# One two-bank PSUM place for the logits of a pair of heads, instead of three one-bank places

## The chip, the cores and the metric
The kernel runs on one core of a Trainium2 chip. The core has TensorE (PE, matrix products), VectorE (DVE), ScalarE (ACT) and GpSimd (POOL), each with its own queue of instructions that it takes in order, SyncE (SP) and other queues for transfers, and 16 DMA engines. Results of matrix products land in PSUM, eight banks of 128 partitions x 512 numbers of 32 bits, and are read from there by DVE or ACT. The metric is the device time of one execution in microseconds.

## The reference, cut to what matters
A sequence of 512 tokens of width 1024 passes through four layers, two of a first and two of a second kind.

```
for i in range(2):                     # first block
    a = gqa(q, k, v)                   # 4 query heads, 2 kv heads, 64 wide, all 512 keys
    b = bidirectional_ssd(...)
    c = softmax(q1 k1 + bias) v - lam * softmax(q2 k2 + bias) v   # 4 heads, 32 wide
    d = spatial_gating(...)
    x = x + merge(a, b, c, d, gates) @ w_out
    x = x + expert_choice_moe(x)       # 16 experts, 64 tokens each, 1024 wide
    x = x + sigmoid(x @ w_ple_gate) * (p @ w_ple)
for l in range(2):                     # second block, 8 heads of 64, causal
    s = sum_h iw[h] * relu(iq[h] . ik) # 4 index heads choose 128 keys a query
    a = softmax over the chosen keys
    b = window attention (128 keys back, 2 kv heads, a sink a head)
    c = stick breaking: beta[t,s] * prod_{s<j<t} (1 - beta[t,j])
    x = x + gate * (merge(a, b, c, gates) @ w_out)
return rms_norm(x)
```

All of it is float32. A projection is computed as three products of rounded halves (xh wh, xl wh, xh wl).

## The kernel before, in words
The program is written with tiles from pools. A pool has so many places under a tag (`bufs`); a tile that finds all places taken waits until the last reader of an earlier one is done, and the waits come from that by themselves. A scheduler sets the order on each engine: it follows the program's order as a priority, which `with self.ahead(n)` raises by n, and its own reckoning of when operands are ready. What it sets is fixed: at run time each engine takes its queue in that order, and an instruction that waits holds up those behind it.

The eight banks of PSUM are given out under three tags (L41 to L43, L122 to L129): `mm` three (projections, in the trace pj, pt, br, and experts), `at` two (transposes tp, products with v, small results), `lg` three, each with one 128x512 tile: the logits lg of the softmax attentions, z of the stick attention, ix of the index heads, and half of the experts' up-products.

Two heads of a pair j = 0, 1 lie on partitions 0 to 63 and 64 to 127 of one tile, so that a logits matmul has 64 rows. For a block of 128 queries (qb) each of these stages makes the logits of both heads, reads them from PSUM, forms the softmax or the sticks, transposes the probabilities (pn, sbb) by PE and multiplies them by v:
The grouped attention (gqa, L616 on; its q and k are qkT): logits over 512 keys, DVE's row maximum, ACT's exponential straight from PSUM. 8 pairs a layer.
The difference attention (L676 on; qks): the two maps m = 0, 1 of a head, 96 rows each (three products of 32 rows stacked); DVE's operation at L709 adds the bias, takes the maximum and writes e to memory. 32 matmuls a layer.
The selected and the window attention (soft_pair, L1492, called for both; names ak, aq and bk, bq): 128 to 512 and 128 to 256 keys; DVE reads them like that. 16 pairs a layer each.
The stick attention (L1594 on; ck, cq): 128 to 512 keys; ACT reads z twice (sba, sbb), POOL masks, DVE multiplies along the row. 16 pairs a layer.
The index scores (L1467 on): four heads for each of three query blocks, read by ACT.
The stages' work is interleaved by the scheduler with projections of stages before and after. The profile gives each PE operation the line of its helper (L153 for matmuls, L157 for transposes), so operations are told apart by the tiles' names.

## Time and profile before
| what | value |
|---|---|
| time, median of 3 runs (lowest to highest) | 3566.06 us (3564.95 to 3567.53) |
| profiled execution: its own time | 3565.2 us |
| its span, first to last instruction | 3563.5 us |
| mean granted clock of TensorE | 0.985 of full speed |
| busy: PE, DVE, ACT, POOL | 96%, 51%, 32%, 12% of the span |

A view by windows gives the busy time of each engine within a stretch of the span; a timeline gives single runs of like instructions (x4 means four records; a 64-row float32 matmul is recorded as two passes, so x2 is one and x4 are two of them). A run's duration is from the start of its first to the end of its last record, so that neighbours overlap a little. "PEclk" is the clock that PE was granted, 1.00 for 2.4 GHz and 0.50 for 1.2.

### The profile page before, as it was taken

Reading aid. Unit: us, or ns where it says so; the run is one execution under the profiler, and the core shown is the slowest. Engines: PE = TensorE matmul, PEld = TensorE weight load, DVE = VectorE, ACT = ScalarE, POOL = GpSimd, SP = SyncE. Lnnn points to the kernel's source line nnn. Section 1 sums busy time; section 2 is a strip of 40 time slices with the busy share of each in tenths; the row PEclk is TensorE's granted clock in tenths of the full one; section 3 lists DMA queues with packets and bytes.
Section 4 is the critical chain, followed back from the end, with each engine's and each line's share of the span. In section 5 each row is a group of like instructions: output and inputs, shape, how many; then the busy total and the mean of one; then the engine's idle time right before and its main releaser. Section 6 shows DMA issues by size and latency. Waiting matters only on the chain. (4 is left out here: it accounts for less than half of the span.)

```text
span 3563.5 us, 42081 instructions
## 1 busy us (share of the span) xinstructions
PE 3430.4 (96%) x15961; PEld 2298.0 (64%) x15961; DVE 1806.6 (51%) x3533; ACT 1133.5 (32%) x2209; POOL 419.1 (12%) x646
## 2 busy tenths in 40 slices
PE   8999999999999999999999999899999999999998
PEld 7867774443437877776434436676678877676887
DVE  7567652111117776673111115697644459756344
ACT  4344641000104444562000113225433322544333
POOL 0110421000000120151000000330210013103000
PEclk9999999999999999999999999899999999999999
DMA  5233667999993233465999985231123332221322
GB/s 177 73 88 108 199 216 282 385 387 388 376 378 109 66 111 105 149 231 202 388 373 402 380 353 226 71 101 62 46 76 103 102 116 76 79 71 36 107 95 71
DMA packets 315437, 655.97 MB, mean 184 GB/s; under 512 B 31075, under 2 KB 208575, under 8 KB 280931
## 3 DMA queue, kind: packets, MB, share of 16 engines
q1 hardware_dynamic: 291968, 628.78, 48.1%
q0 software_dynamic: 8192, 15.22, 1.7%
q10 hardware_dynamic: 15075, 9.29, 0.9%
q8 instruction: 126, 2.06, 0.2%
q14 instruction: 76, 0.62, 0.1%
HBM read 629.59 MB, written 14.70 MB: 181 GB/s over the span
## 5 line engine op out<-in xcount | busy, mean ns | idle before, releaser
L153 PE MATMUL pj<-xh,wh 128*128 128x512 f32 x1808 | 728.1, 404 | 14.3 <-DVE gb L150 6.4
L153 PE MATMUL pj<-xh,wl 128*128 128x512 f32 (+1 forms) x1808 | 725.1, 402 | 10.7 <-DVE wl L142 10.7
L153 PE MATMUL pj<-xl,wh 128*128 128x512 f32 (+1 forms) x1808 | 724.8, 401 | 0.9 <-DVE xl L150 0.7
L132 ACT ACTIVATE wh<-wst 128x1024 fp32r<-128x1024 f32 (+2 forms) x368 | 339.0, 930 | 754.2 <-PE pj L153 570.0
L142 DVE TENSOR_TENSOR wl<-wst,wh 128x1024 fp32r<-128x1024 f32 (+2 forms) x368 | 413.4, 1126 | 308.1 <-ACT wh L132 307.6
L153 PEld LDWEIGHTS pj<-xh,wh 128*128 128x128 f32 x1808 | 342.0, 189 | 110.0 <-DVE gb L150 9.6
L153 PEld LDWEIGHTS pj<-xh,wl 128*128 128x128 f32 (+1 forms) x1808 | 342.0, 189 | 102.7 <-DVE wl L142 13.7
L153 PEld LDWEIGHTS pj<-xl,wh 128*128 128x128 f32 (+1 forms) x1808 | 341.9, 189 | 94.2 <-issue 12.8
L153 PE MATMUL eg<-wst,xe 128*64 128x512 f32 x1008 | 293.0, 596 | 0.0
L153 PE MATMUL eg<-we,xe 128*64 128x512 f32 x560 | 228.4, 596 | 0.0
L153 PEld LDWEIGHTS eg<-wst,xe 128*64 128x64 f32 x1008 | 94.6, 136 | 134.1 <-issue 125.5
L142 DVE TENSOR_TENSOR x<-x,sct 128x512 f32<-128x512 f32 x128 | 83.8, 684 | 187.6 <-PE sct L153 187.6
L142 DVE TENSOR_TENSOR hd<-sg,eg 128x512 f32<-128x512 f32 x32 | 21.9, 685 | 309.0 <-PE eg L153 242.8
L153 PE MATMUL ey<-wst,ht 128*64 128x512 f32 x512 | 161.1, 599 | 7.4 <-DVE ht L139 3.9
L272 POOL TENSOR_TENSOR rr<-msb,mhalf 128x4 f32<-128x4 f32 x9 | 9.2, 1021 | 1344.9 <-DVE msb L146 1344.9
L153 PE MATMUL pt<-wh,xh 128*128 128x256 f32 x512 | 145.9, 285 | 1.4 <-DVE ro L142 1.2
L153 PE MATMUL pt<-wl,xh 128*128 128x256 f32 x512 | 145.1, 283 | 0.0
L153 PE MATMUL pt<-wh,xl 128*128 128x256 f32 x512 | 145.0, 284 | 0.0
L132 ACT ACTIVATE e<-e,nm 128x512 f32<-128x512 f32 (+3 forms) x192 | 111.2, 581 | 70.9 <-DVE nm L146 70.4
L1391 POOL TENSOR_TENSOR wada<-wada 128x1024 f32<-128x1024 f32 (+1 forms) x48 | 101.8, 2121 | 131.5 <-ACT wada L132 129.6
L153 PE MATMUL ey<-we,ht 128*64 128x512 f32 x256 | 115.3, 597 | 1.5 <-DVE ht L139 0.8
L153 PEld LDWEIGHTS eg<-we,xe 128*64 128x64 f32 x560 | 68.2, 136 | 74.2 <-issue 65.2
(495 smaller groups left out, 5788.9 us busy)
## 6 DMA issues: line engine op xcount, KB each, us to landing
wst<-in_w_in_dram SPq DMA_DIRECT2D x90, 1024.0 KB, 5.3
wst<-in_w_exp_gate_dram SPq DMA_DIRECT2D x66, 1024.0 KB, 8.6
wst<-in_w_exp_down_dram SPq DMA_DIRECT2D x64, 1024.0 KB, 11.1
wst<-in_w_exp_up_dram SPq DMA_DIRECT2D x60, 1024.0 KB, 7.8
wst<-in_w_branch_gate_dram SPq DMA_DIRECT2D x32, 1024.0 KB, 5.6
wada<-in_w_ada_dram SPq DMA_DIRECT2D x24, 1024.0 KB, 5.2
we<-in_w_exp_up_dram SPq DMA_DIRECT2D x88, 256.0 KB, 7.1
we<-in_w_exp_down_dram SPq DMA_DIRECT2D x80, 256.0 KB, 9.1
```

Of the source, the lines that this page charges most:

```text
L132: return self.nc.scalar.activation(out, in_, func, **kw)
L142: return self.nc.vector.tensor_tensor(out, a, b, op=op)
L153: return self.nc.tensor.matmul(out, lhsT, rhs, start=start, stop=stop, **kw)
L272: self.nc.gpsimd.tensor_tensor(r, ms, self.mhalf[:, :n], op=OP.pow)
L1391: nc.gpsimd.tensor_tensor(t[:, :k], t[:, :k], t[:, k:2 * k], op=OP.add)
```

## The change
The tag `lg` gets one place of two banks, and a function `lg2` that returns its two halves; `at` gets three places, so that PSUM holds 3 + 3 + 2 banks. The tiles that were single users of `lg` (the input's transposes, the transposes before the experts, those of the output) go to `at`. In the grouped, selected, window and stick attention and in the index scores the two matmuls of a pair are now written first, and both reads behind them; in the grouped and the stick attention with a raised priority (60 and 40). In the difference attention the two maps use the two halves, but stay written as matmul, read, matmul, read.

```diff
@@ -39,8 +39,8 @@
 NA = 10
 NP = 3
 NPM = 3
-NPL = 3
-NPA = 2
+NPL = 1
+NPA = 3
 
 
 def consts():
@@ -125,8 +125,10 @@
     def at(self, name):
         return self.ps.tile([P, S], FT, name=name, tag="at", bufs=NPA)
 
-    def lgp(self, name):
-        return self.ps.tile([P, S], FT, name=name, tag="lg", bufs=NPL)
+    def lg2(self, name):
+
+        t = self.ps.tile([P, 2, S], FT, name=name, tag="lg", bufs=NPL)
+        return t[:, 0], t[:, 1]
 
     def act(self, out, in_, func, **kw):
         return self.nc.scalar.activation(out, in_, func, **kw)
@@ -626,12 +628,12 @@
             for qb in range(NB):
                 es = []
                 mx, nm, ss, rs = (self.sa(n, 2) for n in ("mx", "nm", "ss", "rs"))
-                lg = []
+                lg = self.lg2("lg")
+                with self.ahead(60):
+                    for j in range(2):
+                        self.mat(lg[j], qkT[kv][j * 64:j * 64 + 64, qb * P:qb * P + P], qkT[2 + kv][j * 64:j * 64 + 64, :])
                 for j in range(2):
-                    ps = self.lgp("lg")
-                    self.mat(ps, qkT[kv][j * 64:j * 64 + 64, qb * P:qb * P + P], qkT[2 + kv][j * 64:j * 64 + 64, :])
-                    nc.vector.tensor_reduce(mx[:, j:j + 1], ps, axis=AX.X, op=OP.max)
-                    lg.append(ps)
+                    nc.vector.tensor_reduce(mx[:, j:j + 1], lg[j], axis=AX.X, op=OP.max)
                 self.ts(nm, mx, -0.125, OP.mult)
                 for j in range(2):
                     e = self.ae("e")
@@ -702,8 +704,9 @@
                     off = 384 - qb * P
                     es = []
                     mx, nm, ss, rs, r2 = (self.sa(n, 2) for n in ("mx", "nm", "ss", "rs", "r2"))
+                    lg = self.lg2("lg")
                     for m in range(2):
-                        ps = self.lgp("lg")
+                        ps = lg[m]
                         self.mat(ps, w[:, 0, m, qb * P:qb * P + P], w[:, 1, m])
                         e = self.ae("e")
                         nc.vector.tensor_tensor_reduce(e, ps, sv[:, j, 384 - off:896 - off][:, ::-1], scale, GONE, OP.add, OP.max, mx[:, m:m + 1])
@@ -1239,11 +1242,11 @@
                 side.append(lambda g4=g4, d2=d2, nx=nxt: gather(g4, d2, nx))
             xc = pr % 2 * P
             pss = []
-            for pool in (self.mm, self.lgp):
-                two = [pool("eg%d" % i) for i in range(2)]
+            for _ in range(2):
+                two = self.lg2("eu") if pss else [self.mm("eg%d" % i) for i in range(2)]
                 for k2 in range(4):
                     ts = [take() for j in range(2)]
-                    if pr == 0 and pool == self.mm:
+                    if pr == 0 and not pss:
                         gather(0, k2, xs)
                     for k in range(2):
                         kt = k2 * 2 + k
@@ -1474,9 +1477,11 @@
             nk = (qb + 1) * P
             acc = hold[:, qb * S - S:qb * S]
             for h in range(4):
-                ps = self.lgp("ix")
-                r = h % 2 * 64
-                self.mat(ps[:, :nk], iq[h // 2][r:r + 64, qb * P:qb * P + P], ik[r:r + 64, :nk])
+                if h % 2 == 0:
+                    two = self.lg2("ix")
+                    for j in range(2):
+                        self.mat(two[j][:, :nk], iq[h // 2][j * 64:j * 64 + 64, qb * P:qb * P + P], ik[j * 64:j * 64 + 64, :nk])
+                ps = two[h % 2]
                 t = self.ae("ixr")
                 self.act(t[:, :nk], ps[:, :nk], AF.Relu)
                 self.stt(acc[:, :nk], t[:, :nk], iw[:, qb * 4 + h:qb * 4 + h + 1],
@@ -1495,13 +1500,14 @@
         n = len(kts) * P
         mx, nm, ss, rs = (self.sa(x, 2) for x in ("mx", "nm", "ss", "rs"))
         es = []
+        lg = self.lg2("lg")
         for j in range(2):
             r = j * 64
-            ps = self.lgp("lg")
-            self.mat(ps[:, :n], q[r:r + 64, qb * P:qb * P + P], k[r:r + 64, kts[0] * P:kts[0] * P + n])
+            self.mat(lg[j][:, :n], q[r:r + 64, qb * P:qb * P + P], k[r:r + 64, kts[0] * P:kts[0] * P + n])
+        for j in range(2):
             e = self.ae("e")
             init = GONE if sink is None else sink[:, t * 2 + j:t * 2 + j + 1]
-            nc.vector.tensor_tensor_reduce(e[:, :n], ps[:, :n], mask, 0.125, init, OP.add, OP.max, mx[:, j:j + 1])
+            nc.vector.tensor_tensor_reduce(e[:, :n], lg[j][:, :n], mask, 0.125, init, OP.add, OP.max, mx[:, j:j + 1])
             es.append(e)
         self.ts(nm, mx, -1.0, OP.mult)
         for j in range(2):
@@ -1609,10 +1615,13 @@
             pts = [self.pt("ptc%d" % j) for j in range(2)]
             for qb in range(NB):
                 n = (qb + 1) * P
+                zz = self.lg2("z")
+                with self.ahead(40):
+                    for j in range(2):
+                        r = j * 64
+                        self.mat(zz[j][:, :n], q[t][r:r + 64, qb * P:qb * P + P], k[t][r:r + 64, :n])
                 for j in range(2):
-                    r = j * 64
-                    z = self.lgp("z")
-                    self.mat(z[:, :n], q[t][r:r + 64, qb * P:qb * P + P], k[t][r:r + 64, :n])
+                    z = zz[j]
                     a, b = self.ae("sba"), self.ae("sbb")
                     q1 = self.sb.tile([P, S + 4], FT, name="sbq", tag="ae", bufs=NA)
                     self.act(a[:, :n], z[:, :n], AF.Sigmoid, scale=-1.0)
```

The order on the engines shows what this does. First PE in the selected attention (lg from the tiles ak and aq, among projections pj and bv and transposes tp of the probabilities pn), before:

```order
L153 MATMUL lg<-ak_15497,aq_15493 128x256 [waits DVE_49]
L153 MATMUL bv<-xh,wl 128x512
L153 MATMUL bv<-xh,wh 128x512
L153 MATMUL lg<-ak_15497,aq_15493 128x384 [waits DVE_49]
L153 MATMUL bv<-xl,wh 128x512
L153 MATMUL bv<-xh,wl 128x512
L153 MATMUL pj<-xh,wh 128x512 [waits Activation_49]
L153 MATMUL pj<-xl,wh 128x512
L153 MATMUL pj<-xh,wl 128x512 [waits DVE_49]
```

and after:

```order
L155 MATMUL pj<-xl,wh 128x512
L155 MATMUL pj<-xh,wl 128x512
L155 MATMUL lg<-ak_15433,aq_15429 128x384 [waits DVE_49]
L155 MATMUL lg<-ak_15433,aq_15429 128x384
L155 MATMUL pj<-xh,wh 128x512
L155 MATMUL pj<-xl,wh 128x512
L155 MATMUL pj<-xh,wl 128x512
L155 MATMUL pj<-xh,wh 128x512
```

Single logits matmuls, each with a wait of its own for DVE, have become two in a row, of which only the first waits.

PE at the first head pair of the stick attention (z from ck and cq; tp of sbb are the transposes of the sticks), before:

```order
L153 MATMUL z<-ck_17758,cq_17754 128x256 [waits Activation_49]
L153 MATMUL z<-ck_17758,cq_17754 128x384 [waits Activation_49]
L157 MATMUL tp<-ident,sbb 128x128 [waits DVE_49,PE_49]
L153 MATMUL z<-ck_17758,cq_17754 128x384 [waits Activation_49]
L157 MATMUL tp<-ident,sbb 128x128 [waits DVE_49,PE_49]
L157 MATMUL tp<-ident,sbb 128x128 [waits DVE_49,Activation_49]
L157 MATMUL tp<-ident,sbb 128x128 [waits Pool_49]
L153 MATMUL z<-ck_17758,cq_17754 128x512
L157 MATMUL tp<-ident,sbb 128x128 [waits DVE_49,PE_49]
L157 MATMUL tp<-ident,sbb 128x128 [waits Pool_49]
L153 MATMUL z<-ck_17758,cq_17754 128x512 [waits Activation_49]
```

and after:

```order
L155 MATMUL z<-ck_17656,cq_17652 128x384 [waits Activation_49]
L155 MATMUL z<-ck_17656,cq_17652 128x384
L159 MATMUL tp<-ident,sbb 128x128 [waits DVE_49,PE_49] x3
L159 MATMUL tp<-ident,sbb 128x128 [waits Pool_49]
L155 MATMUL pj<-xh,wh 128x512
L155 MATMUL pj<-xl,wh 128x512
L159 MATMUL tp<-ident,sbb 128x128 [waits DVE_49,Activation_49]
L159 MATMUL tp<-ident,sbb 128x128 [waits Pool_49]
L155 MATMUL pj<-xh,wl 128x512
L155 MATMUL pj<-xh,wh 128x512
L155 MATMUL pj<-xl,wh 128x512
L155 MATMUL pj<-xh,wl 128x512
```

The two heads' z, which had transposes between them, stand together, and the wait for ACT (the reader of z) is on the first alone; projections (pj) stand between the transposes.

PE in the difference attention (lg from qks; pj and br are projections of the merge that runs beside it), before:

```order
L153 MATMUL lg<-qks 128x512 [waits DVE_49]
L153 MATMUL pj<-xh,wh 128x512 [waits Activation_49]
L153 MATMUL pj<-xl,wh 128x512
L157 MATMUL tp<-ident,pn 128x128 [waits DVE_49,PE_49]
L157 MATMUL tp<-ident,pn 128x128 x3
L153 MATMUL br<-odh,bh 128x512
L153 MATMUL lg<-qks 128x512 [waits DVE_49]
L153 MATMUL br<-odl,bh 128x512
```

and after:

```order
L155 MATMUL lg<-qks 128x512 [waits DVE_49]
L159 MATMUL tp<-ident,pn 128x128 [waits DVE_49,PE_49]
L159 MATMUL tp<-ident,pn 128x128 x3
L155 MATMUL lg<-qks 128x512 [waits DMASW3_49,DMASW2_49,DMASW6_49,DMASW1_49,DMASW7_49,DMASW0_49,DVE_49]
L155 MATMUL lg<-qks 128x512 [waits DVE_49]
L159 MATMUL tp<-ident,pn 128x128 [waits DVE_49,Activation_49]
L159 MATMUL tp<-ident,pn 128x128 x3
L155 MATMUL lg<-qks 128x512 [waits DVE_49]
```

At the change of head two logits matmuls now stand one behind the other, each with a wait for DVE. On DVE itself, in the same stage, the reads of the logits (e, mx from lg and the bias strip) with what stands around them, before:

```order
L146 TENSOR_SCALAR pn<-e,rs 128x512
L709 ISA e,mx<-lg,strip 128x512
L709 ISA mx 128x1
L150 SCALAR_TENSOR_TENSOR pn<-e,r_2624,pn 128x512 [waits DVE_49]
L709 ISA e,mx<-lg,strip 128x512
L709 ISA mx 128x1
```

and after:

```order
L148 TENSOR_SCALAR pn<-e,rs 128x512
L712 ISA e,mx<-lg,strip 128x512 [waits PE_49]
L712 ISA mx 128x1
L152 SCALAR_TENSOR_TENSOR pn<-e,r_2615,pn 128x512 [waits DVE_49]
L712 ISA e,mx<-lg,strip 128x512 [waits PE_49]
L712 ISA mx 128x1
```

The order is the same; the two reads had no wait for PE there, since both matmuls were known to be done, and each has one now.

## Rows read from the trace of the kernel before

**Rows 1.** The page: span and busy times of the engines.
```profile
span 3563.5 us, 42081 instructions
PE 3430.4 (96%) x15961; PEld 2298.0 (64%) x15961; DVE 1806.6 (51%) x3533; ACT 1133.5 (32%) x2209; POOL 419.1 (12%) x646
```

**Rows 2.** Windows by stage: window, length, PE, PEld, DVE, ACT, POOL, PEclk, DMA, GB/s.
```profile
195.00:245.00 50.00, 49.84 (x218) 29.68 (x218) 33.67 (x74) 23.76 (x52) 3.55 (x7) 1.00 0.16 45
275.00:390.00 115.00, 112.67 (x516) 86.86 (x516) 92.43 (x214) 56.39 (x115) 1.67 (x1) 1.00 0.40 130
557.00:1078.00 521.00, 506.83 (x2128) 217.60 (x2125) 89.63 (x152) 52.92 (x89) 0.31 (x1) 1.00 0.95 375
2296.00:2384.00 88.00, 81.17 (x432) 67.81 (x430) 85.23 (x192) 17.14 (x26) 28.45 (x44) 0.96 0.28 83
2384.00:2443.00 59.00, 58.26 (x270) 36.04 (x270) 43.59 (x148) 30.40 (x84) 5.92 (x9) 1.00 0.16 47
2443.00:2523.00 80.00, 79.59 (x398) 53.91 (x398) 55.70 (x208) 42.18 (x129) 0.15 (x1) 1.00 0.24 79
2549.00:2606.00 57.00, 53.70 (x236) 27.70 (x236) 48.70 (x85) 33.59 (x86) 29.65 (x95) 0.94 0.00 1
2556.70:2563.50 6.80, 6.45 (x19) 3.35 (x21) 5.49 (x10) 3.18 (x9) 3.70 (x11) 0.50 0.00 0
```

**Rows 3.** Timeline of PE, single runs of logits: start, duration, operation.
```profile
200.05 1.13 PE L153 MATMUL lg<-qkT,qkT 64*128 64x512 f32 x4
...
221.69 1.12 PE L153 MATMUL lg<-qkT,qkT 64*128 64x512 f32 x2
...
2445.90 0.48 PE L153 MATMUL lg<-bk,bq 64*128 64x128 f32 x2
...
2447.68 0.70 PE L153 MATMUL lg<-bk,bq 64*128 64x256 f32 x2
...
2451.72 0.70 PE L153 MATMUL lg<-bk,bq 64*128 64x256 f32 x4
...
2553.33 0.91 PE L153 MATMUL z<-ck,cq 64*128 64x384 f32 x2
```

**Rows 4.** Windows of tile lg alone: grouped (two layers), before, selected, window attention.
```profile
195.00:245.00 50.00, 12.26 (x32) 3.93 (x32) 10.79 (x16) 11.56 (x32) 1.00 0.16 45
1299.00:1347.00 48.00, 11.90 (x32) 3.63 (x28) 10.77 (x16) 11.54 (x32) 1.00 0.16 46
2347.00:2384.00 37.00, 0.92 (x6) 0.52 (x6) 0.01 (x1) 0.00 (x0) 1.00 0.29 82
2384.00:2443.00 59.00, 18.52 (x60) 7.50 (x60) 13.27 (x30) 0.00 (x0) 1.00 0.16 47
2443.00:2523.00 80.00, 17.08 (x63) 7.73 (x62) 14.91 (x34) 0.00 (x0) 1.00 0.24 79
```

**Rows 5.** Windows of tile z alone, stick attention of two layers.
```profile
2549.00:2606.00 57.00, 22.43 (x64) 8.16 (x64) 0.00 (x0) 24.86 (x64) 0.00 (x0) 0.94 0.00 1
3207.00:3264.00 57.00, 22.92 (x64) 8.53 (x64) 0.00 (x0) 24.84 (x64) 0.00 (x0) 0.94 0.00 1
```

**Rows 6.** Timeline of PE: projections behind a logits matmul.
```profile
2390.93 0.50 PE L153 MATMUL pj<-xh,wl 128*128 128x512 f32 x1
2391.27 0.40 PE L153 MATMUL pj<-xh,wh 128*128 128x512 f32 x1
2391.50 0.39 PE L153 MATMUL pj<-xl,wh 128*128 128x512 f32 x1
```

**Rows 7.** Timeline of PE: a logits matmul of the difference attention.
```profile
288.24 0.40 PE L153 MATMUL lg<-qks 96*128 96x512 f32 x1
```

**Rows 8.** Timeline of DVE in the difference attention, between two reads.
```profile
286.49 0.75 DVE L150 SCALAR_TENSOR_TENSOR pn<-e,r,pn 128x512 f32<-128x512 f32 x1
287.15 0.68 DVE L709 CUSTOM_DVE_ANT_0 e<-lg,strip 128x512 f32<-128x512 f32 x1
```

**Rows 9.** Waits, 2549 to 2606: who for whom, total, times, longest.
```profile
PEld z L153 <- issue: 3.3, 12, 0.8
```

More of the change, by code (lines that the diff above doesn't have):

```diff
@@ L395, in setup @@
         for k in range(KT):
-            ps = self.at("xps") if k % 2 else self.lgp("xps")
+            ps = self.at("xps")
             for tb in range(NB):
@@ L1152, in moe @@
             for tb in range(NB):
-                ps = self.lgp("h2t")
+                ps = self.at("h2t")
                 for k in range(4):
@@ L1681, in final @@
         for tb in range(NB):
-            self.copy(o[0][:, tb], turn(0, tb, self.lgp("ops")))
+            self.copy(o[0][:, tb], turn(0, tb, self.at("ops")))
         r = self.rms_cols()
-        pss = [turn(1, tb, self.mm("opm") if tb % 2 else self.lgp("ops")) for tb in range(NB)]
+        pss = [turn(1, tb, self.mm("opm") if tb % 2 else self.at("ops")) for tb in range(NB)]
         for tb in range(NB):
```

## Prediction
> **What bounds the kernel now.** I read the page's busy times first: TensorE (PE) is busy 3430.4 of 3563.5 us, VectorE (DVE) about half of that [rows 1]. A share of the whole span hides stages with different limits, so next come windows cut by stage [rows 2]. In their order: the grouped attention (195 to 245), the difference attention (275 to 390), the experts (557 to 1078), the index scores with their top-k (2296 to 2384), then in the second block the selected attention (2384 to 2443), the window attention (2443 to 2523) and the stick-breaking attention (2549 to 2606). The reader is to see three limits. In the attention stages PE is busy all but a little of the time and DVE has room: there a shorter PE program is a shorter kernel. The experts run with the DMA engines busy 0.95: PE time is worth nothing there. In the index stretch DVE works 85.23 of 88 us: it decides. The stick stage is its own case: PE 53.70 of 57, DVE 48.70, and in 6.8 us of it PE runs at half clock (1.2 GHz), last row of [rows 2].
>
> Then I looked at single logits matmuls on PE [rows 3]. A head has 64 rows, so two heads of a pair stand on different halves of the partitions. Two matmuls of 512 columns that follow each other (x4: each is recorded as two passes) take 1.13 us; one alone (x2) takes 1.12. At 256 columns it is 0.70 for two and 0.70 for one. So a pair runs side by side and costs what one costs. With three single places most second heads wait for a place of their own and come later, alone: that is what the change can take away.
>
> **What is removed: lone logits matmuls.** In the order of PE after the change the second matmul stands directly behind the first with no wait in 16 of 16 pairs of the grouped attention's two layers, 32 of 32 of the window attention, 30 of 32 of the selected and 28 of 32 of the stick attention. The sums per layer, from the durations of [rows 3] (0.48 for 128 columns, 0.70 for 256, 0.91 for 384, 1.12 for 512):
> Grouped attention: 8 pairs x 1.13 = 9.0 instead of 12.26 and 11.90 [rows 4]: 3.2 + 2.9 = 6.1 us for both layers.
> Selected and window attention: now 0.92 + 18.52 + 17.08 = 36.5 [rows 4]. After: 4 x (0.48 + 0.70 + 0.91 + 1.12) + 0.70 for a split pair = 13.5, and 4 x 0.48 + 12 x 0.70 = 10.3. Saved 12.7 a layer, 25.3 in two.
> Stick attention: now 22.43 and 22.92 [rows 5]. After: 4 x 3.21 + 1.18 for two split pairs = 14.0. Saved 8.4 and 8.9, 17.3.
> Sum 48.7 us, all of it on an engine that these stages wait for.
>
> **Fewer changes of shape.** Behind a 64-row matmul the next projection matmul starts, and the one behind it starts 0.34 us later, where the usual step is 0.23 [rows 6]: about 0.1 us is lost each time PE leaves a run of such matmuls. In PE's order these runs fall from 158 to 118: 40 x 0.1 = 4 us saved. Bounds 0 and 40 x 0.2 = 8.
>
> **What moves.** With `ahead` the scheduler issues the stick logits earlier than their program order, and it moves projection work into the stick stage: in PE's order the stage grows from 132 to 213 instructions. PE has 57 - 53.70 = 3.3 us idle in it [rows 2], in two layers 6.6; with projections at hand between pairs I count it as filled. Bounds 0 and 6.6. The half-clock windows (3.4 us lost in each of two layers, if at full clock the same work needed half of 6.8) may stay or vanish; PE was waiting in short steps before the clock fell, and I take 0, bounds 0 and 7 gained.
>
> **What is added: a wait.** One place for two logits means that the first matmul of a pair waits until the last read of the pair before. Where both matmuls are issued together I let projections cover that wait: they stand between the pairs in PE's order. The difference attention is different. Its code still issues matmul, read, matmul, read, its matmuls have 96 rows and don't pair, and the two halves of the place are watched as one: each matmul waits for the read just before it, where formerly it waited for the read three back. The chain from one read to the next is then: PE's issue after a wait, about 0.28 (3.3 / 12 [rows 9]), and the matmul 0.40 [rows 7], together 0.68, against 0.66 from 286.49 to 287.15 in which DVE works on the multiply-add between [rows 8]. The cover just fails; PE is moreover in the middle of another instruction of about 0.40, half of it on average 0.2. So 0.25 for each second read: 32 in two layers, 8 us. What is queued behind the waiting matmul on PE are projections and transposes that had nothing to wait for, and DVE has 23 us of room there, so I count the delay as PE's. Below: nothing, if PE always comes late anyway; above: every one of 64, 16 us. At the change of head two matmuls stand directly one behind the other, the second waiting for the read of the first (0.28 + 0.68): twice a layer, 4 us for the kernel.
> The places of the experts' up-products, of the transposes and of the final output change too. The experts are hidden by the DMA engines; the others are few: 0, bounds -3 and +3. The index pairs save PE time where DVE decides: 0, bounds -2 and +2.
>
> **Sum.** -48.7 - 4 - 6.6 + 8 + 4 = -47.3. Against the profiled execution's 3565.2 that is 3517.9; the median of the runs shown is 0.9 above it, so 3519.
>
> **The rivals.**
> First: the readers take over. The faster PE waits for the engines that empty PSUM. By rows, in the stick stage DVE has 48.70 us of work, and with 16 hand-offs of 0.28 it can't be shorter than 53.2: it gives 3.8 a layer instead of 8.6 + 3.3. That takes 16 of my 47 away: -31, 3535. For it: the single place ties logits to readers. Against it: in the other stages DVE is at 33.67 of 50, 43.59 of 59, 55.70 of 80 [rows 2], with 25% to spare. The Trainium skill, TensorEngine Tiling (Array Packing), Performance Considerations, has this as a rule: tiling speeds up TensorE but not the emptying of PSUM, which may become the bottleneck. By it the time is 3535; no row before the change shows a stage in which that has happened. Chance 0.2.
> Second: the change does not do what it says. The matmuls stand together but a write to the other bank of one place doesn't start beside the first. Then only the runs and the idle time are won, and the difference attention's 12 are lost: 3563 to 3567. Against it: pairs in the kernel before run side by side also from banks next to each other. 0.06.
> Third, slower: the wait at the hand-off. A pair can't start before the last read of the pair before is done, and PE, which takes its instructions in order, stands still until then. There are 112 hand-offs of pairs (16 + 32 + 32 + 32) and 64 in the difference attention. Without my 12 for the latter the gain is 59; shared by 176 hand-offs the point of decision is 0.34 us each. At 0.45 it costs 79, a loss of 20: 3585. Against it: one cycle of a pair fits well in its stage. In the stick stage four activations of 0.39 (24.86 / 64 [rows 5]), the pair of 0.9 and two hand-offs of 0.28 make 3.0, where 57 / 16 = 3.6 are to be had; in the grouped attention two reads and two exponentials of 0.7, the pair of 1.1 and three hand-offs make 4.8 of 6.3. 0.06.
> Fourth: more. The half-clock windows go (7), the difference attention is hidden (12): 3500. 0.15.
> My forecast has 0.53.
>
> **How the numbers follow.** The low end 3494 is the fourth case and the upper bounds of runs and small places; the high end 3552 holds the first rival with the difference attention at its upper bound (3535 + 8) and some 9 for pairs split by the clock's moves in time. Left out are the second and third rivals and a third of the fourth: 0.17. About 0.2% or 7 us is what a measurement of this kernel can tell from no change. Faster by more: 0.53 + 0.2 + 0.15 and none of the second, 0.88. The second gives nearly all of no change, 0.05; slower is the third and what is left, 0.07.
>
> **What would show it.** Right: 64-row logits in runs of x4 with the duration of a x2 now; the logits' PE time near 9 us in the grouped attention, 24 in selected and window together, 14 in stick; the end of the second block's attention some 21 us a layer earlier; the difference attention up to 6 us a layer longer with PE waiting for DVE's read at the logits. Wrong: lone x2 logits as frequent as now; PE idle before logits at the pairs, released by ScalarE's or DVE's reads; the stick stage no shorter than 53 us at equal content, with DVE without a gap; or the experts' stages changing at all.

## The result, and the profile after

The changed kernel takes 3508.69 us (median of 4 runs, 3505.55 to 3509.70), the kernel before 3565.51 in the same comparison: a ratio of 0.9838, 95% interval 0.9821 to 0.9855, 57 us faster. The forecast was 3519, 47 us faster. The total is close, but it is the sum of errors of opposite sign, and that they nearly cancel is luck: the experts' stages, which I put at nothing, gave 43 us, and the second block gave 28 of the 49 us that I put there (logits and filled idle time). The page after, which answers to [rows 1]:

```profile
span 3506.4 us, 42089 instructions
PE 3355.4 (96%) x15961; PEld 2274.0 (65%) x15961; DVE 1809.8 (52%) x3533; ACT 1133.2 (32%) x2209; POOL 422.3 (12%) x646
```

PE does the same 15961 records in 75 us less, and its idle time grows by 18 (133 us before, 151 after); the other engines do what they did. Where that falls is seen from the starts of operations that both traces have. Lengths of five stretches, first layer / second layer of their block, worked out from those starts (us):

```
stretch (from .. to)                                        before        after
M grouped attention .. router (first qkt to first rlg)    339.7/338.1   343.0/342.6   +7.8
E experts (first slt to the next norm's ms)               539.2/541.1   517.5/520.2  -42.6
I index and top-k (iwt to first bk)                       112.8/113.6   113.3/113.4   +0.3
A selected and window attention (first bk to first z)     177.3/177.5   163.8/164.5  -26.5
S stick attention and merges (first z to last merge / to output)
                                                          297.0/341.7   296.6/340.8   -1.3
everything else                                                                       +5.0
```

Two of these stretches do not hold the same work before and after. In each layer 35 records of a projection (pt, 4.9 us of PE) moved from A into S, so that at equal content A gained some 8 us a layer and S some 5.5. And 12 records of a projection (pj, 2.8 us) moved from each expert stage into the stretch behind it, so that E gained some 37 us at equal content.

**The logits did what was worked out.** Windows of the tiles lg and z alone on PE, columns as in [rows 4, 5]: grouped attention, selected with window attention, and stick attention of both layers.

```profile
193.00:243.00 50.00, 8.20 (x30) 2.11 (x28) 10.52 (x16) 11.55 (x32) 1.00 0.24 66
...
2318.00:2480.00 162.00, 23.72 (x128) 9.62 (x124) 27.57 (x62) 0.00 (x0) 1.00 0.25 75
```
```profile
2506.00:2564.00 58.00, 13.79 (x64) 5.10 (x62) 0.00 (x0) 22.84 (x62) 0.00 (x0) 1.00 0.06 19
3151.00:3209.00 58.00, 14.12 (x64) 5.39 (x64) 0.00 (x0) 22.59 (x62) 0.00 (x0) 1.00 0.06 19
```

23.7 us where 13.5 + 10.3 = 23.8 were predicted, 13.8 and 14.1 where 14.0 were, 8.2 where 9.0 were (two of the 32 records start before this window; all 32 take 9.03 in either layer). In PE's timeline the pairs now read x4 at the duration of the x2 in [rows 3]:

```profile
2423.89 0.70 PE L155 MATMUL lg<-bk,bq 64*128 64x256 f32 x4
...
2512.66 0.92 PE L155 MATMUL z<-ck,cq 64*128 64x384 f32 x4
```

**The stick stage.** Its window after, with the clock at 1.00 where it was 0.94:

```profile
2506.00:2564.00 58.00, 51.55 (x273) 30.80 (x271) 46.74 (x82) 31.52 (x85) 28.78 (x91) 1.00 0.06 19
```

It holds 37 records more than in [rows 2], since projections were moved in, and it isn't the same piece of work: from the first to the last z there are 47.6 us and 189 records before, 56.9 us and 270 records after. PE is idle for 58 - 51.55 = 6.5 us in it, where 3.3 were idle before and I had none left. ScalarE's wait for logits and PE's wait for the finished sticks (sbb) have grown; before, in 2549 to 2606:

```profile
ACT sba L132 <- PE z L153: 5.7, 9, 2.3
...
PE tp L157 <- DVE sbb L142: 2.1, 3, 0.9
```
and after, in 2506 to 2564:
```profile
ACT sba L134 <- PE z L155: 19.1, 14, 3.2
...
PE tp L159 <- DVE sbb L144: 5.7, 10, 1.3
```

So most of PE's idle time there, 5.7 of 6.5 us, ends with a stick that VectorE finished.

**The experts.** Their window, as in [rows 2], now moves 391 GB/s with the DMA engines 0.98 busy, against 375 and 0.95:

```profile
558.00:1058.00 500.00, 484.66 (x2120) 214.86 (x2119) 87.82 (x151) 52.56 (x88) 0.31 (x1) 1.00 0.98 391
```

PE's idle time in this window did not fall: 521 - 506.83 = 14.2 us before, 500 - 484.66 = 15.3 after. Its busy time fell, by 22 us at nearly the same records. Before the change PE hardly waited for weights either: in 557 to 1078 its weight loads waited 3.8 us in sum for transfers, the matmuls themselves never; the largest entry:

```profile
PEld eg L153 <- DMA wst<-in_w_exp_up_dram: 0.8, 3, 0.3
```

One part of what changed is read from the scatter products (sct: each expert result is multiplied into an `at` place, and VectorE adds it to x, L142 before, L144 after). Instruction groups by line (durations in ns as minimum/median/maximum, then the first and last start), and the waits of PE and of its weight loads for that addition; before:

```profile
L153 PE MATMUL sct<-oht,yh x64: 387/494/505, 613.2 to 1076.3; 128*128 128x512 f32 x64
...
PEld sct L153 <- DVE x L142: 10.9, 16, 1.2
...
PE sct L153 <- DVE x L142: 4.9, 12, 0.8
```
and after:
```profile
L155 PE MATMUL sct<-oht,yh x64: 388/400/506, 615.6 to 1055.7; 128*128 128x512 f32 x64
...
PEld sct L155 <- DVE x L144: 5.3, 10, 1.0
PE sct L155 <- DVE x L144: 0.6, 1, 0.6
```

From the first scatter to the last there are 463.1 us before and 440.1 after. PE's own wait for VectorE's addition is nearly gone, and PE is busy for less time with the same scatters (tile sct alone, 56 of the 64), before and after:

```profile
560.00:1050.00 490.00, 39.40 (x112) 18.22 (x112) 36.77 (x56) 1.00 0.96 379
```
```profile
560.00:1050.00 490.00, 34.69 (x112) 18.69 (x112) 35.74 (x56) 1.00 0.99 394
```

In steps from the start of one PE operation to the start of the next, worked out from the trace of the first layer, those that end at a scatter sum to 51.5 us before and 41.4 after: 10 of the stage's 21.7 us, half of them idle time. Another 10.7 lie in the steps of the gate and up products (246.7 us before, 236.0 after), of which 6.5 are lost again before the transposes of their results (hdt). Why those products step faster isn't shown. In PE's order the scatters of both layers stand in 65 runs, before in 84, and the expert products between them are cut into fewer pieces (144, before 162). The shorter scatter doesn't come from that: its median is 400 ns with three places (here and in e1) and 486 to 494 with two (before, e2, and e5 with 70 runs).

**The difference attention.** PE around one change of head, from the timeline with its idle time in brackets:

```profile
287.22 0.40 PE L155 MATMUL br<-odh,bl 128*128 128x512 f32 x1
288.33 0.49 PE L155 MATMUL lg<-qks 96*128 96x512 f32 x1 [0.71 <-DVE mx L712]
289.08 0.63 PE L159 MATMUL tp<-ident,pn 128*128 128x128 f32 x4 [0.26 <-DVE pn L152]
289.61 0.50 PE L155 MATMUL lg<-qks 96*128 96x512 f32 x1
293.29 0.80 PE L155 MATMUL lg<-qks 96*128 96x512 f32 x1 [3.18 <-DVE mx L712]
294.05 1.09 PE L159 MATMUL tp<-ident,pn 128*128 128x128 f32 x4
294.88 0.79 PE L155 MATMUL lg<-qks 96*128 96x512 f32 x1
295.63 0.79 PE L155 MATMUL pj<-xh,wh 128*128 128x512 f32 x1
```
```profile
293.20:299.20 6.00, 5.87 (x14) 3.67 (x15) 4.53 (x10) 3.52 (x6) 0.00 (x0) 0.52 0.07 25
```

The matmul at 289.61 is the second head's first map, the one at 293.29 its second. The second waits 3.18 us for VectorE to read the first, in the same place (3.78 us in the second layer; there is one such change of head a layer). VectorE has other work in its queue before that read, of the merge (bl, macc) and of the softmax of the pair before (from its timeline):

```profile
290.14 0.69 DVE L144 TENSOR_TENSOR bl<-wst,bh 128x512 fp32r<-128x512 f32 x1
290.75 0.69 DVE L144 TENSOR_TENSOR macc<-macc,gb 128x512 f32<-128x512 f32 x1
291.82 0.17 DVE L717 RECIPROCAL rs<-ss 128x2 f32<-128x2 f32 x1 [0.39 <-ACT e L134]
...
292.55 0.68 DVE L712 CUSTOM_DVE_ANT_0 e<-lg,strip 128x512 f32<-128x512 f32 x1
```

The hand-off itself is short: that read ends at 292.55 + 0.68 = 293.23, and the matmul starts at 293.29. Behind the idle stretch PE runs at half clock (0.52 granted in the next 6 us, second fence; 0.50 in the second layer): projections take 0.79 instead of 0.40. Over the stage the granted clock is 0.97, where [rows 2] has 1.00:

```profile
273.00:388.00 115.00, 109.22 (x481) 81.10 (x480) 87.82 (x205) 54.27 (x111) 1.67 (x1) 0.97 0.36 118
```

### The profile page after: what moved, and what is told of

It is laid out like the page before. It is cut to its first block, busy times and chain, and to the rows that moved or that the text cites. A ratio compares the mean times of both kernels' runs of the same rounds, so it can differ in the third digit from the quotient of the medians.

```text
span 3506.4 us, 42089 instructions
## 1 busy us (share of the span) xinstructions
PE 3355.4 (96%) x15961; PEld 2274.0 (65%) x15961; DVE 1809.8 (52%) x3533; ACT 1133.2 (32%) x2209; POOL 422.3 (12%) x646
## 4 chain that ended last, share of the span: by engine, by line
PE 66%; issue 16%; DVE 9%; POOL 3%; ACT 3%; DMA 2%; ACTq 0%; POOLq 0%; DVEq 0%; SPq 0%
PE pj L155 27%; PE ey L155 7%; PE eg L155 6%; PE eu L155 4%; PE br L155 4%; PE pt L155 3%; PE av L155 2%; PE xe L155 2%; PE tp L159 2%; PE lg L155 2%; PE sct L155 2%; DVE wl L144 1%; DVE sel L1492 1%; PE pw L155 1%; DVE m L1491 1%
## 5 line engine op out<-in xcount | busy, mean ns | idle before, releaser
L144 DVE TENSOR_TENSOR wl<-wst,wh 128x1024 fp32r<-128x1024 f32 (+2 forms) x368 | 415.5, 1132 | 290.7 <-ACT wh L134 288.5
L155 PEld LDWEIGHTS pj<-xh,wl 128*128 128x128 f32 (+1 forms) x1808 | 341.7, 189 | 95.9 <-DVE wl L144 10.7
L155 PEld LDWEIGHTS pj<-xl,wh 128*128 128x128 f32 (+1 forms) x1808 | 342.8, 190 | 93.9 <-issue 10.1
L144 DVE TENSOR_TENSOR hd<-sg,eu 128x512 f32<-128x512 f32 x32 | 21.9, 685 | 338.4 <-PE eu L155 225.5
L155 PE MATMUL eg<-wst,xe 128*64 128x512 f32 x528 | 158.1, 597 | 0.0
L144 DVE TENSOR_TENSOR x<-x,sct 128x512 f32<-128x512 f32 x128 | 81.2, 682 | 133.9 <-PE sct L155 133.9
L155 PE MATMUL eu<-wst,xe 128*64 128x512 f32 x480 | 130.6, 593 | 1.3 <-DMA wst<-in_w_exp_up_dram 1.3
L155 PE MATMUL eu<-we,xe 128*64 128x512 f32 x288 | 117.9, 593 | 0.2 <-DMA we<-in_w_exp_up_dram 0.2
L155 PE MATMUL eg<-we,xe 128*64 128x512 f32 x272 | 116.6, 598 | 0.0
```

The lines of the kernel that those rows point to most:

```text
L144: return self.nc.vector.tensor_tensor(out, a, b, op=op)
L155: return self.nc.tensor.matmul(out, lhsT, rhs, start=start, stop=stop, **kw)
```

## The experiments

Each run's time stands against runs of the kernel before on the same chip (3564 to 3566 us in all of them). The stretches M, E, A and S are those of the table above.

**e1: the third place alone.** The kernel before with
```diff
-NPL = 3
-NPA = 2
+NPL = 2
+NPA = 3
```


> The kernel before, with the third place for small results taken from the logits (logits two single places, no pairs written together). Theory A, a third place for small results shortens the experts' stages: the two expert stages lose 18 to 21 us each as in the changed kernel, while the attentions gain nothing, since singles stay singles: 3526 to 3540. Rival B, the two-bank place of the up-products did it: the expert stages keep their 540 us, and the whole stays at 3560 to 3580.

Measured: 3555.03 us, ratio 0.997 (0.9959 to 0.9981). E is 521.0/525.2: 34 us of the 43, with PE's wait at the scatters as short as in the changed kernel:
```profile
PEld sct L153 <- DVE x L142: 5.8, 10, 1.0
PE sct L153 <- DVE x L142: 0.9, 2, 0.5
```
The whole is slower than A's range, because the attentions with two single places lost 21 us (A 181.3/181.3, S 303.5/348.1). The third place for small results is the larger part of the experts' gain. The rest, some 4 us a layer, came only with the two-bank place; why was not tested, and e6 shows that an expert stage whose code is unchanged can differ by 2 to 6 us between two versions.

**e2: without the third place.** The changed kernel with
```diff
-NPA = 3
+NPA = 2
```


> The changed kernel with two places for small results instead of three (one bank unused). Theory A: both expert stages grow by 18 to 21 us, the attentions keep their gain: 3545 to 3553. Rival B: the expert stages stay short, 3507 to 3515.

Measured: 3549.24 us, ratio 0.9952 (0.9937 to 0.9967), 41 above the changed kernel, in A's range. E goes back to 537.8/534.6 (the 12 projection records of each stage go back too, 5.6 us of this), and the waits to 10.7 and 4.3. A is 168.0/167.4: the pairs keep 9 to 10 of their 13 us there with two places.

**e3: half of the scatters elsewhere.** The kernel before with
```diff
-            ps = self.at("sct")
+            ps = self.at("sct") if i % 2 else self.lgp("sct")
```


> The kernel before, with every other scatter product of the experts in a place of the logits (of whose three the experts use only two), nothing else changed. Theory A1, it is the scatter that waits for a place that VectorE is still reading: PE's time at the scatters falls from 47 to about 39 us a layer and the two expert stages shorten by 14 to 21 us each, 3525 to 3540. Rival A2, the third place works through the other small results or through how the scheduler groups the scatters (their runs on PE stay near 80 here, against 65 in the changed kernel): under 6 us a stage, 3555 to 3566.

Measured: 3571.12 us, ratio 1.0017 (1.0008 to 1.0027), E 536.8/538.6, which the 12 projection records that left each stage here too account for. A1 fell in this form: places lent from the logits' rotation, in which the up-products turn too, don't help, and PE's wait at the scatters stayed (5.0 us, before 4.9). A2's stages came true, the whole lies 5 us above its range. Why the lent place doesn't help is open; e10 and e11 show by another way that the scatters depend on their places.

**e4: pairs undone in two attentions.** The changed kernel with
```diff
             self.mat(lg[j][:, :n], ...)
-        for j in range(2):
             e = self.ae("e")
```


> The changed kernel, in which the selected and the window attention are again written as matmul, read, matmul, read, in the two-bank place. Theory, lone matmuls cost their full time on a PE that decides: the logits of the two stages rise from 24 to 37 us a layer or more, and with a hand-off before every matmul another 0 to 10 us a layer: 3531 to 3550. Rival, the stages have slack on PE and pairing there bought nothing: 3506 to 3514.

Measured: 3568.19 us, ratio 1.0013 (1.0004 to 1.0023): 59 above the changed kernel, and above both theories' ranges. A is 197.2/195.9, 33 us a layer longer. The window of lg alone, first layer:
```profile
2352.00:2550.00 198.00, 45.78 (x120) 18.03 (x119) 28.50 (x60) 0.00 (x0) 0.96 0.17 54
```
All 64 logits matmuls are alone now; at the durations of [rows 3] that is 2 x (12.84 + 10.32) = 46.3 us, as measured, against 23.7 in pairs. So 22 of the 33 us are the pairs; of the rest 3 are more idle time on PE, and what remains lies in slower projections and products around (the clock fell to 0.96 here). One place without pairs is worse than three single places without them (A 177.3): the change pays by its order and the place together.

**e5: scatters in twos, two places.** The kernel before with
```diff
-                for d in range(4):
-                    side.append(lambda i=dh * 4 + d, ...: scatter(i, yh, yl, oht))
+                for d in range(0, 4, 2):
+                    side.append(lambda i=dh * 4 + d, ...: [scatter(i + u, yh, yl, oht) for u in range(2)])
```


> The kernel before, with the experts' scatter products written two at a time between the steps of the weights instead of one at a time; places unchanged. On PE the runs of scatters fall from 84 to 70 (65 in the changed kernel), the pieces into which they and the others cut the expert products from 162 to 154 (144). Theory G, each cut of the expert products costs PE, whatever the number of places: the two expert stages (539 and 541 us) shorten by 8 to 15 us each, 3535 to 3550. Rival P, what cost was the scatter's wait for a place that VectorE still reads: two at a time need two places at once, so PE's idle time before scatters grows from 5.8 us a stage and the stages shorten by 0 to 4 us or lengthen, 3557 to 3575.

Measured: 3555.23 us, ratio 0.9975 (0.9964 to 0.9987), E 537.1/533.4: 2.1 and 7.7 us shorter. Below G in both layers, and between the two ranges as a whole; the waits for the addition stayed (10.1 and 4.5 us). Fewer cuts alone are worth little, if anything, not the 20 us: untouched stages differ by up to 6 us in e6.

**e6: both maps of the difference attention first.** The changed kernel with
```diff
                     for m in range(2):
+                        self.mat(lg[m], w[:, 0, m, ...], w[:, 1, m])
+                    for m in range(2):
                         ps = lg[m]
-                        self.mat(ps, w[:, 0, m, ...], w[:, 1, m])
                         e = self.ae("e")
```


> The changed kernel, with both matmuls of the difference attention written first and both reads behind them. Theory, its two hand-offs a pair cost 4 to 7 us a layer (idle 4.0 before logits, logits 1.7 longer) and one of the two goes: the stretch from the grouped attention to the merge's end (343.0 and 342.6 us) shortens by 2 to 5 us a layer, 3498 to 3505. Rival, the wait only moves, because the first matmul then waits for the second read: 3506 to 3512.

Measured: 3498.76 us, ratio 0.9813 (0.9798 to 0.9828), within the theory's range. M falls to 340.0/339.4, 3.1 us a layer. The waits at the logits in 271 to 390, in the changed kernel:
```profile
PEld lg L155 <- DVE mx L712: 5.9, 7, 3.5
PE lg L155 <- DVE mx L712: 3.9, 2, 3.2
```
in the kernel before:
```profile
PEld lg L153 <- DVE mx L709: 2.0, 5, 1.2
PE lg L153 <- DVE mx L709: 0.7, 1, 0.7
```
and here:
```profile
PEld lg L155 <- DVE mx L713: 0.2, 1, 0.2
```
The wait goes, and the stage's clock rises to 0.99. The cost of the hand-off is thereby shown: 6 us for both layers, of the 14 that M lost. Some 4 of the 10 us lie in the experts' stages (519.8/514.3), which this edit doesn't touch; such a difference between runs of one stage I don't explain.

**e7: one read of the stick logits instead of two.** The changed kernel with
```diff
-                for j in range(2):
-                    z = zz[j]
-                    a, b = self.ae("sba"), self.ae("sbb")
+                aa = [self.ae("sba") for j in range(2)]
+                for j in range(2):
+                    self.act(aa[j][:, :n], zz[j][:, :n], AF.Sigmoid, scale=-1.0)
+                for j in range(2):
+                    a, b = aa[j], self.ae("sbb")
...
-                    self.act(a[:, :n], z[:, :n], AF.Sigmoid, scale=-1.0)
-                    self.act(b[:, :n], z[:, :n], AF.Sigmoid)
+                    self.act(b[:, :n], a[:, :n], AF.Copy, scale=-1.0, bias=1.0)
```


> The changed kernel, in the stick attention of which ScalarE reads each logits tile once instead of twice, both heads first, and forms beta as one minus the other from memory: the place comes free after two activations of 0.39 us on average instead of four, the work of the engines being nearly the same. Theory H, the hand-off of the single place holds the stick stage (ScalarE waited 19.1 us for logits, before 5.7): up to 16 x 0.78 = 12 us a layer, I expect 5 to 8 a layer, 3492 to 3500. Rival C, the chain through GpSimd, VectorE and the transposes holds it: 3504 to 3512, with ScalarE waiting as long but for other things.

Measured: 3516.97 us, ratio 0.9868 (0.9848 to 0.9889), slower than the changed kernel; S is 302.1/346.6, 5.6 us a layer longer. The gain of theory H did not come: ScalarE's wait for logits did shrink, but PE's waits before the transposes grew (the wait for sbb was 5.7):
```profile
PEld tp L159 <- issue: 10.0, 10, 2.3
ACT sba L134 <- PE z L155: 7.7, 8, 3.0
...
DVE sbq L1634 <- POOL sba L1631: 6.9, 7, 2.6
PE tp L159 <- DVE sbb L144: 6.7, 6, 1.7
```
ScalarE waited less and the stage didn't use it. What is waited for is the chain behind the logits: GpSimd's mask, VectorE's scan (sbq) and product (sbb), then the transposes. The test is not a clean one, though: the edit also puts beta behind the other activation, PE's order changed with it, and the clock fell to 0.94 in 2514 to 2572, which alone is worth about 58 x 0.06 = 3.5 of the 5.6 us.

**e8: stick logits at ordinary priority.** The changed kernel with
```diff
-                with self.ahead(40):
+                with self.ahead(0):
```


> The changed kernel, with the stick logits at their ordinary priority: on PE they stand in 56 runs instead of 36, so that few pairs stay together. Theory H, the stage waits for the hand-off and not for PE's time: the 8 us that pairs save on PE are not worth 8, but later logits lengthen the hand-off: 3508 to 3520, with ScalarE waiting longer than 19 us for logits. Rival, PE decides in the stick stage: two layers x 8.5 lone logits more, 3525 to 3530.

Measured: 3541.53 us, ratio 0.9936 (0.9919 to 0.9953), more than either theory. S is 309.8/354.2, 13 us a layer longer; A is 4 to 5 longer, because the 35 projection records stand there again. Theory H's sign failed: ScalarE waits 12.4 us for logits in 2509 to 2586, not over 19. So PE's time does count in this stage: lone logits cost 8.9 us a layer on PE (22.1 us from start to start, 13.2 in pairs), while PE's idle time in S grew by 2.4 and 3.5. That S got no shorter in the changed kernel is therefore not because PE has no part in it: it saved 8 us at the logits and some 3 with the half clock gone, took in 4.9 us of other work, and its idle time grew by 4.2.

**e9: maps first and scatters in twos.** e6 with the edit of e5:

> The changed kernel with both maps of the difference attention first (as in the run above, 3498.8) and the experts' scatters two at a time, now with three places for them: on PE their runs fall from 65 to 54, the pieces of the expert products from 144 to 136. If cuts cost while places are at hand, the expert stages shorten by another 3 to 8 us each: 3484 to 3494. If with three places the scatters were already free, nothing: 3496 to 3502.

Measured: 3496.94 us (5 runs), ratio 0.9803 (0.9790 to 0.9816), which can't be told from e6. E is 519.3/518.9. That is what was expected if the scatters were already free with three places. These two are the fastest versions here.

**e10 and e11: the three banks split.** The changed kernel with
```diff
-NPA = 3
+NPA = 2      # e11: 1
-            ps = self.at("sct")
+            ps = self.ps.tile([P, S], FT, name="sct", tag="sc", bufs=1)   # e11: 2
```


> The changed kernel, in which the three banks for small results are split: one place for the scatters alone, two for the rest. If the scatters need more than one place at once (each waits for VectorE to add the one before), the expert stages grow to 545 us or more, with idle time before scatters above 6 us a stage. If it was the other small results that lacked a place, the stages stay near 520.

> The changed kernel, with the three banks split the other way: two places for the scatters alone, one for the rest (transposes and products with v in the attentions too, which get slower; only the expert stages are read). If two free places for the scatters are what the third bank gave, the stages stay at 517 to 527 us. If the other results need two places, they grow to 535 or more, with waits before transposes and gathers rather than before scatters.

One run each: 3636.09 and 3659.74 us (e11's transposes and small products have one place everywhere). E is 578.7/575.9 and 557.6/552.9. PE's waits at the scatters, e10:
```profile
PEld sct L155 <- DVE x L144: 31.4, 28, 1.2
PE sct L155 <- DVE x L144: 22.1, 28, 0.9
```
and e11:
```profile
PEld sct L155 <- DVE x L144: 9.6, 14, 1.0
PE sct L155 <- DVE x L144: 4.3, 12, 0.5
```
Both answers cover the first 56 scatters; over all 64 of the layer PE waits 23.1 us with one place of its own, 5.0 with two, against 4.9 with two shared (before) and 0.6 with three shared (after). My reading of e11 as either-or was wrong: with two places of their own the scatters wait as they did before, and the stage is 12 to 18 us longer than before, so that one place seems too few for the others as well; which of them wait was not followed up.

**e12: two places of two banks.** The changed kernel with
```diff
-NPM = 3
-NPL = 1
-NPA = 3
+NPM = 2
+NPL = 2
+NPA = 2
```


> The changed kernel with two two-bank places for the logits, paid by the projections (two places instead of three) and the small results (two instead of three); read by stages. If the hand-off of the single place holds the stick stage, PE's idle time in it falls from 6.1 to under 4 us a layer and ScalarE's wait for logits from 19 to under 10 us, and in the difference attention the idle time before logits falls from 4.0 to under 1.5 us. If the chain through the other engines holds the stick stage, its idle time stays at 5 us or more. The whole is 3530 to 3600, since the experts fall back to two places for small results.

One run: 3618.19 us. The difference attention's wait stayed:
```profile
PEld lg L155 <- DVE mx L712: 7.1, 10, 4.0
PE lg L155 <- DVE mx L712: 4.3, 2, 3.7
```
That wait hangs on the order in the code (matmul, read, matmul, read within one watched place) and not on the number of places, as e6 shows from the other side. In the stick stage (2590 to 2650) ScalarE waits 14.9 us for logits and PE idles 4.7 us between its first and last z, against 6.1 (5.9 in the second layer, against 6.2): between the two theories in one layer, at the chain's value in the other, and with fewer pairs together (42 runs instead of 36), so it decides nothing.

## Why the prediction was right in the sum, and wrong in its steps

**Lone logits removed**: right, to within 0.2 us a term of PE's busy time, in all four attentions; e4 undoes it in two of them and costs 59 us. Not all of it became time: in selected and window attention the steps from start to start at the logits shrank by 11.1 us a layer, not 12.7, and idle time and slower steps around them took 2.7 of that.

**Fewer changes of shape, 4 us**: not seen. The products with v and the merge products between them took 2.8 us a layer more in the second block (29.6 for 28.1, 68.0 for 66.7 from start to start), which cancels it.

**Idle time of the stick stage filled, 6.6 us**: wrong. PE's idle time there rose from 3.3 to 6.5 us a layer. This is close to my first rival, confined to one stage: the engines behind the logits keep their own pace, though not as it was worded, since it isn't the emptying of PSUM that holds PE. ScalarE, which alone empties z, works 22.84 of 58 us on it, and 5.7 of PE's 6.5 us idle end with a stick from VectorE, whose work takes 46.74 of the 58; that this chain sets the stage is read from the waits, and no run shows it by itself. The Trainium skill, TensorEngine Tiling (Array Packing), Performance Considerations, says that the PSUM copy may become the bottleneck after a fourfold speedup of TensorE. In none of the four attentions does this trace show that. The half-clock windows of [rows 2] went, as my fourth rival had it (the stage's window shows 1.00): 3.4 us a layer by the prediction's working.

**The difference attention, 12 us**: M grew by 7.8 us although the logits of the grouped attention saved 6, so 14 us were lost: the size right, partly by luck. I put 8 of the 12 on a delay of 0.25 for every second read, with 0.28 for each hand-off from [rows 9], a row of issue time and not of hand-offs. The trace shows 0.06 at the hand-off above, and only 2.1 us of such waits in both layers. The change of head I had right in kind but not in size: one long wait a layer (3.18 and 3.78 us, where I had 0.96 twice), because other work stands ahead of the read in VectorE's queue, and the half clock behind it. e6 removes the wait and wins back 6 us; of the other 8 no run shows the cause.

**The experts, 0 with bounds of 3**: wrong, and the largest error: -42.6 us. I took a DMA share of 0.95 for a limit. It left 26 us of 521 unused in each stage, PE was busy 0.97 of it, and PE's matmuls never waited for a transfer: PE set the pace, and the transfers went faster when its work shrank. The prediction had named any change of these stages as a sign of being wrong, and so it was. A sign was in the waits: PE waited at the scatters for VectorE's addition, 12 times in a layer, its weight loads 16 times. But those 4.9 us are no price for what came of it, since shorter scatters and faster gate and up products make up the rest. e1 and e2 turn the effect on and off with the third place, e10 and e11 give the waits with one and two places; the way from the place to the time is shown for the scatters alone, about half of it.

Five us were given back elsewhere, 2.4 and 4.0 of them in the stretch behind each expert stage (from its end to the next layer's attention), into which the 12 projection records (2.8 us each time) had moved.

## What to carry to other kernels

A shared pool's extra place is worth reading at every user of its tag, in particular where a producer and an adder turn through it: ask how often PE waits there for the place, and whether PE waits for the transfers, not how busy the DMA engines are. The wait is a sign and not a price: here 4.9 us of it in a layer stood for a gain of some 18. Two half-height matmuls of a pair are worth writing next to each other in one place, so that only the first waits; but then both must be issued before either is read, or the place makes each wait for the other's reader. In a stage whose other engines form a chain of their own, part of what PE saves comes back as idle time. And before two stages are compared, count their records: the scheduler may have moved work from one to the other.

## What was not expected of the hardware

Behind an idle stretch of 3.18 us between matmuls the granted clock was 0.52, nearly all of it at 1.2 GHz, for the next 6 us. By estimate that costs 6 x 0.48 = 2.9 us of PE's work, so that the wait cost about as much again as it lasted. In the stick stage the reverse was seen: PE paused more often and longer (13 pauses, 6.1 us in all, the longest 1.28, where it had 10, 3.3 us and 0.93), and the clock stayed at 1.00, where it had been 0.94. These runs don't show why it fell there before.
